# The last output block of a decoder step's down projection: token columns in three groups instead of two, and the place of one scaling

## The chip, the cores and the metric

The kernel runs on one core of a Trainium2 chip. The metric is the device time of one execution in microseconds (us), as the median of several runs. Engines are named as in the profile: PE is TensorE (PEld its weight loads), DVE is VectorE, ACT is ScalarE, POOL is GpSimd, SP is SyncE, which issues most DMAs.

## The reference, cut to what matters

The reference is one step of a hybrid decoder on 512 prompt tokens and 8 sample tokens: a mixer of mLSTM and retention heads, cross-attention, a SwiGLU block and a final RMSNorm. The change touches the end only:

```
x = x + (silu(hf @ w_gate) * (hf @ w_up)) @ w_down        # w_down: 2816 x 1024
y = x * rsqrt(mean(x * x, over the 1024 features) + EPS) * g_final
```

Tokens do not mix here: each token's row of y needs all 1024 features of its own x, and nothing of other tokens.

## The kernel before, in words

Features stand on the 128 partitions and the 520 tokens on the free axis, so the 1024 features are 8 blocks (KB) of 128 by 520. X holds the residual stream. Float32 precision comes from three products of rounded halves: high weight by high input, high weight by low input, low weight by high input. Each product has its own 128x128 stationary tile, a slice of `whi` or `wlo`, and a moving tile from A or TT (the two places that hold the 22 blocks of the SwiGLU output). Two products in a row may use the same slice of `whi`, but each is issued with a weight load of its own.

The down projection goes through its 8 output blocks in turn. Blocks 0 to 6 (L1269 to L1287) multiply both token halves, 0 to 260 and 260 to 520, and then add the result to X (L1285), square it into the running sum `ssq` (L305, L306) and scale the block by the final norm's weights (L1287). Block 7 is written apart (L1289 to L1326): 66 products (22 blocks by 3) for tokens 0 to 260, then 66 for tokens 260 to 520. The three pairs of weight chunks are kept from the first half (`chunks`). The chunks are transferred and split as before this block, in the pace of the block ahead.

When a half's products are done, generators named `finish` take over. A `finish` for a group of n tokens

- sums `ssq` over the partitions by a product with a tile of ones into `pn` (L1294),
- adds the products to X (L1295), squares block 7 (L1297) and adds that square's sum to `pn` (L1299),
- makes the reciprocal root in `rsqrt_rows`: Ln on ACT (L277), the mean `nrmv` on DVE (L278), Exp on ACT (L279), three DVE steps on `r` (L280 to L282),
- scales block 7 by the norm's weights on ACT (L1302),
- multiplies X by `r` into FR in three pieces of 3, 3 and 2 feature blocks (L1305), each followed by its DMA out, on the queues of SP, ACT and SP (L1306).

The groups that `finish` serves are given by `CUTS`: tokens 0 to 260, 260 to 390 and 390 to 520. The first half has one `finish`. The second half's 66 products serve two, which start together when the last product is done. The pieces of a `finish` are threaded between the products by `step()`. A scheduler at build time sets the order on each engine; engines keep that order when they run, and `keep_in_program_order` pins an instruction to the place where the code has it.

Of the kernel before, what the change touches and what calls it, by code (L numbers as in the profile page):

```python
# [13 lines left out]
AF = mybir.ActivationFunctionType  # L14
# [11 lines left out]
KB = 8  # L26
T = 512
NS = 8
N = T + NS
H2 = N // 2  # L30
# [23 lines left out]
V_BUF, V_WC, V_BC, V_GMIX, V_GX, V_GF, V_GM, V_GH, V_GO = 0, 24, 28, 29, 30, 31, 32, 33, 34  # L54
# [86 lines left out]
def decoder_step(ctx: ExitStack, tc: tile.TileContext, i: dict, o: list):  # L141
    nc = tc.nc
    pe, act, dve, pool, sp = nc.tensor, nc.scalar, nc.vector, nc.gpsimd, nc.sync
# [18 lines left out]
    def ps2(name):  # L162
        return acc.tile([P, 2, 512], F32, tag="acc", name=name)

    def ps1(name):
        return psums[-1].tile([P, 512], F32, tag="msc", name=name)
# [4 lines left out]
    vec = main.tile([P, KB, NV], F32, name="vec")  # L171
# [57 lines left out]
    def spawn(gen, group=None):  # L229
        tasks.append([gen, 0, group])  # L230

    def step():

        for t in list(tasks):
            t[1] -= 1
            if t[1] <= 0:
                try:
                    t[1] = next(t[0]) or 2
                except StopIteration:
                    tasks.remove(t)  # L240
# [5 lines left out]
    def proj(x, name, order=range(KB), ahead=1):  # L246
        hi, lo = W.get(ahead)
        ps = ps2(name)
        for n, k in enumerate(order):
            mm_k(ps, hi, lo, x, k, k, n == 0, n == KB - 1)  # L250
            if n % 2 and n < KB - 1:
                step()
        return ps
# [18 lines left out]
    def rsqrt_rows(pl, r, ps):  # L272

        n = ps.shape[-1]
        v = pl.tile([P, N], F32, tag="row", name="nrmv")[:, :n]
        l = pl.tile([P, N], F32, tag="row", name="nrml")[:, :n]
        act.activation(l, ps, AF.Ln, bias=eps_c, scale=1.0 / D)  # L277
        dve.tensor_scalar(v, ps, 1.0 / D, EPS, ALU.mult, ALU.add)  # L278
        act.activation(l, l, AF.Exp, scale=-0.5)  # L279
        dve.tensor_tensor(r, l, l, ALU.mult)  # L280
        dve.scalar_tensor_tensor(r, r, -0.5, v, ALU.mult, ALU.mult)
        dve.scalar_tensor_tensor(r, r, 1.5, l, ALU.add, ALU.mult)  # L282
# [85 lines left out]
    with ExitStack() as mx:  # L368
# [17 lines left out]
        n0 = mp.tile([NS, 4, HD], F32, name="n0")  # L386
# [416 lines left out]
        for hb in range(KB):  # L803
            ps = proj(A, "pgt")
# [60 lines left out]
    for ob in range(KB):  # L865

        ps = proj(B, "pwo", range(KB) if ob < KB - 1 else (*range(4, KB), *range(4)))
# [244 lines left out]
    for (k0, nk, nc_), need in zip(PASSES, (1, 2, 3)):  # L1112
        while min(done[0], attended[0]) < need or any(t[2] == "mem" for t in tasks):
            step()
        for c0 in range(0, D, nc_):
            hi, lo = W.get()
            for c in range(0, nc_, P):
                ob = (c0 + c) // P
                ps = ps2("pwc")
# [6 lines left out]
                else:  # L1126
                    xb = X[:, ob]
# [23 lines left out]
    def ff(s, k, ts):  # L1151
        return A[:, s, k, ts] if k < KB else TT[:, k - KB, s, ts]
# [55 lines left out]
    for f in range(PLAIN):  # L1208
        ps = proj(A, "pfg")
# [9 lines left out]
        ps = proj(A, "pfu", ahead=int(f < PLAIN - 1))  # L1219
# [4 lines left out]
    for f in range(PLAIN, FB):  # L1224
# [5 lines left out]
        ps = [pc, pd, ab[:, 0, :H2], ab[:, 1, :H2], pe_, cd[:, 0, :H2], cd[:, 1, :H2]]  # L1230
# [38 lines left out]
    for obs in ((0, 1), *((ob,) for ob in range(2, KB - 1))):  # L1269
# [13 lines left out]
        for ob, ps in zip(obs, pss):  # L1283
            xb = X[:, ob]
# [4 lines left out]
    xb = X[:, KB - 1]  # L1289
    chunks = []  # L1290
    def finish(ts, n, ps):

        pn = ps1("pn")[:, :n]
        pe.matmul(pn, ones, ssq[:, ts], start=True, stop=False)  # L1294
        dve.tensor_tensor(xb[:, ts], xb[:, ts], ps, ALU.add)  # L1295
        sq7 = yp.tile([P, n], F32, name="sq7", bufs=3)
        act.activation(sq7, xb[:, ts], AF.Square)  # L1297
        yield 1
        pe.matmul(pn, ones, sq7, start=False, stop=True)  # L1299
        r = yp.tile([P, n], F32, name="r", bufs=3)  # L1300
        rsqrt_rows(yp, r, pn)
        act.activation(xb[:, ts], xb[:, ts], AF.Copy, scale=vec[:, KB - 1, V_GO : V_GO + 1])  # L1302
        out = fr[:, KB * ts.start : KB * ts.stop].rearrange("p (k n) -> p k n", n=n)
        for q, k0, k1 in ((sp, 0, 3), (act, 3, 6), (sp, 6, 8)):
            dve.tensor_tensor(out[:, k0:k1], X[:, k0:k1, ts], r.unsqueeze(1).broadcast_to([P, k1 - k0, n]), ALU.mult)  # L1305
            q.dma_start(y[:, KB * ts.start + k0 * n : KB * ts.start + k1 * n].rearrange("p (k n) -> p k n", n=n), out[:, k0:k1])  # L1306

    for n0, n in ((0, H2), (H2, N - H2)):
        ts = slice(n0, n0 + n)
        ps = ps2("pfd")[:, 0, :n]  # L1310
        for k0 in range(0, FB, KB):
            if n0 == 0:
                chunks.append(W.get())
            hi, lo = chunks[k0 // KB]
            for k in range(min(KB, FB - k0)):
                for w, s in ((hi, 0), (hi, 1), (lo, 0)):
                    pe.matmul(  # L1317
                        ps, w[:, k], ff(s, k0 + k, ts),
                        start=k0 + k == 0 and w is hi and s == 0, stop=k0 + k == FB - 1 and w is lo,
                    )  # L1320
            step()
        for c0, c1 in zip(CUTS, CUTS[1:]):
            if ts.start <= c0 < ts.stop:
                spawn(finish(slice(c0, c1), c1 - c0, ps[:, c0 - ts.start : c1 - ts.start]))
        step()
    drain()  # L1326
    yx.close()
# [5 lines left out]
CUTS = (0, H2, H2 + H2 // 2, N)  # L1333
# [61 lines left out]
```

## Time and profile before

| | us |
|---|---|
| median of 3 runs (849.76 to 851.43) | 850.98 |
| the profiled execution's own time | 851.71 |
| its span, first to last instruction | 849.9 |

The span of the profile is what the views below show; 1.8 us of the profiled execution lie outside it (851.71 - 849.9). Times in the rows are counted from the start of the span. Over the whole span PE is busy 97%, DVE 74%, ACT 50%, POOL 19%. The block that the change touches is the last 27 us.

### The profile page before, as it was taken

The page shows a single profiled execution, that of the slowest core. Times are in us where ns is not written, and L with a number is a line of the kernel's source. Part 1 is how long each engine was busy: PE and PEld are TensorE (multiplying, and loading weights), DVE is VectorE, ACT ScalarE, POOL GpSimd, SP SyncE. Part 2 cuts the span into 40 slices and gives each one's busy share as a digit, 9 for nine tenths or more (in the row PEclk, how much of TensorE's full clock was granted, in tenths as well). Part 3 has the DMA queues.
Part 4 walks back from the last instruction along what each step waited for, and adds up shares of the span by engine and source line. Part 5 has one row for each costly group of instructions (what it writes and reads, how often), then busy time and mean ns, then how long its engine had stood idle before and what let it go on. Part 6 is the DMA issues. An engine that isn't in the chain of part 4 may idle for free.

```text
span 849.9 us, 16985 instructions
## 1 busy us (share of the span) xinstructions
PE 824.3 (97%) x6643; PEld 807.6 (95%) x6643; DVE 632.8 (74%) x1393; ACT 426.5 (50%) x871; POOL 163.0 (19%) x282
## 2 busy tenths in 40 slices
PE   6999999999999999899999899999999999999995
PEld 4999999999999999789999899999999999999995
DVE  5999977667676778767888899999999997422234
ACT  6556886556545544356432555555454455332231
POOL 5122422222145301424322500000000000010010
PEclk9999999999999999999999999999999999999999
DMA  8344546444526347784755222333333333333212
GB/s 279 103 131 164 176 168 217 158 138 162 189 76 216 105 127 246 235 287 130 243 196 153 75 58 93 107 113 90 109 113 118 101 99 94 94 106 94 79 59 100
DMA packets 34088, 119.01 MB, mean 140 GB/s; under 512 B 4320, under 2 KB 6560, under 8 KB 32728
## 3 DMA queue, kind: packets, MB, share of 16 engines
q1 hardware_dynamic: 27216, 95.80, 35.9%
q0 software_dynamic: 5024, 20.79, 6.7%
q10 hardware_dynamic: 1768, 1.34, 0.5%
q8 instruction: 52, 0.85, 0.4%
q14 instruction: 28, 0.23, 0.1%
HBM read 108.77 MB, written 9.14 MB: 139 GB/s over the span
## 4 chain that ended last, share of the span: by engine, by line
PE 86%; DVE 6%; DMA 4%; POOL 1%; ACT 1%; issue 1%; SPq 0%; DVEq 0%; POOLq 0%; ACTq 0%
PE pfd L1277 13%; PE pfb L1236 6%; PE pfa L1236 6%; PE pcv L222 6%; PE pgt L222 5%; PE pcq L222 5%; PE pwo L222 5%; PE ppl L222 5%; PE pwc L222 4%; PE pfd L1236 3%; PE pfe L1236 3%; PE pfc L1236 3%; PE prp L222 3%; PE pfu L222 2%; PE pfg L222 2%; PE pfd L1317 1%
## 5 line engine op out<-in xcount | busy, mean ns | idle before, releaser
L207 ACT CAST whi<-wraw 128x1024 fp32r<-128x1024 f32 (+1 forms) x104 | 107.3, 1033 | 167.3 <-PE pfd L1277 58.1
L208 DVE TENSOR_TENSOR wlo<-wraw,whi 128x1024 fp32r<-128x1024 f32 (+1 forms) x88 | 112.6, 1281 | 71.5 <-ACT whi L207 69.5
L306 POOL TENSOR_TENSOR ssq<-ssq,sq 128x520 f32<-128x520 f32 x18 | 29.1, 1618 | 355.6 <-ACT sq L305 355.5
L191 ACT CAST qhi<-wsum 128x512 fp32r<-128x512 f32 x72 | 42.9, 620 | 41.4 <-DVE wsum L1183 26.6
L1277 PE MATMUL pfd<-TT,whi 128*128 128x260 f32 x392 | 62.8, 283 | 0.0
L1277 PEld LDWEIGHTS pfd<-TT,whi 128*128 128x128 f32 x392 | 53.7, 189 | 0.0
L1236 PE MATMUL pfa<-TT,qhi 128*128 128x260 f32 x288 | 53.1, 282 | 0.0
L1236 PE MATMUL pfb<-TT,qhi 128*128 128x260 f32 x288 | 52.8, 283 | 0.0
L208 POOL TENSOR_TENSOR wlo<-wraw,whi 128x1024 fp32r<-128x1024 f32 x16 | 38.4, 2399 | 60.3 <-ACT whi L207 55.2
L191 DVE TENSOR_TENSOR qlo<-wsum,qhi 128x512 fp32r<-128x512 f32 x72 | 48.9, 683 | 0.6 <-ACT qhi L191 0.6
L222 PE MATMUL pwc<-B,whi 128*128 128x260 f32 x256 | 43.8, 287 | 4.0 <-DVE X L295 3.0
L222 PE MATMUL pcv<-A,whi 128*128 128x260 f32 x256 | 44.3, 293 | 1.7 <-ACT whi L207 1.7
L1236 PEld LDWEIGHTS pfb<-TT,qhi 128*128 128x128 f32 x288 | 44.4, 189 | 0.2 <-issue 0.2
L1236 PEld LDWEIGHTS pfa<-TT,qhi 128*128 128x128 f32 x288 | 44.4, 189 | 0.0
L222 PE MATMUL prp<-A,whi 128*128 128x260 f32 x256 | 44.2, 291 | 0.0
L222 PE MATMUL ppl<-A,whi 128*128 128x260 f32 x256 | 42.9, 287 | 0.0
L222 PE MATMUL pgt<-A,whi 128*128 128x260 f32 x256 | 42.7, 289 | 0.0
L222 PE MATMUL pcq<-A,whi 128*128 128x260 f32 x256 | 42.0, 284 | 0.0
L222 PE MATMUL pwo<-B,whi 128*128 128x260 f32 x256 | 41.4, 283 | 0.0
L1236 PE MATMUL pfb<-TT,qlo 128*128 128x260 f32 x144 | 40.8, 283 | 0.0
L222 PEld LDWEIGHTS pwc<-B,whi 128*128 128x128 f32 x256 | 35.8, 189 | 5.1 <-DVE X L295 3.7
L1236 PE MATMUL pfa<-TT,qlo 128*128 128x260 f32 x144 | 40.5, 282 | 0.0
(431 smaller groups left out, 2556.6 us busy)
## 6 DMA issues: line engine op xcount, KB each, us to landing
wraw<-in_weights_dram SPq DMA_DIRECT2D x132, 512.0 KB, 3.8
kqb<-there POOLq DMA_DIRECT2D x8, 1024.0 KB, 5.2
kv<-in_cache_k_dram SPq DMA_DIRECT2D x16, 512.0 KB, 4.3
kv<-in_cache_v_dram SPq DMA_DIRECT2D x16, 512.0 KB, 4.4
wraw<-in_weights_dram SPq DMA_DIRECT2D x8, 384.0 KB, 3.1
X<-in_x_dram SPq DMA_DIRECT2D x2, 1040.0 KB, 5.9
Cs<-in_state_C_dram POOLq DMA_DIRECT2D x4, 512.0 KB, 4.3
out_dram<-Cs POOLq DMA_DIRECT2D x4, 512.0 KB, 3.0
```

Of the source, the lines that this page charges most:

```text
L191: return act.copy(hi, src), dve.tensor_tensor(lo, src, hi.bitcast(F32), ALU.subtract)
L207: act.copy(hi[:, :n], raw[:, :n])
L208: (pool if index in LO_ON_POOL else dve).tensor_tensor(lo[:, :n], raw[:, :n], hi[:, :n].bitcast(F32), ALU.subtract)
L222: pe.matmul(ps[:m, a, :H2], w[:, k, c0 : c0 + m], x[:, s, xk, a * H2 : (a + 1) * H2], start=first and w is hi and s == 0, stop=last and w ...
L306: (dve if ob == KB - 1 else pool).tensor_tensor(ssq, ssq, s, ALU.add)
L1236: pe.matmul(out, w[:, k * P : (k + 1) * P], x[:, k * H2 : (k + 1) * H2], start=k == 0 and w is wh and x is xh, stop=k == 3 and w is wl,)
L1277: pe.matmul(ps[:, a, :H2], w[:, k - k0], ff(s, k, slice(a * H2, (a + 1) * H2)), start=k == 0 and w is hi and s == 0, stop=k == FB - 1 and ...
L1317: pe.matmul(ps, w[:, k], ff(s, k0 + k, ts), start=k0 + k == 0 and w is hi and s == 0, stop=k0 + k == FB - 1 and w is lo,)
```

## The change

Block 7 of the down projection is cut into the three groups of `CUTS` itself. Each group has its own 66 products: 66 of 260 columns, then 66 of 130, then 66 of 130. The former second half of 66 products of 260 columns becomes 132 products of 130. Every group has its own PSUM tile and its own `finish`, started when its products are done. In `finish` the ACT scaling of block 7 (L1302) is kept in program order, which puts it behind Ln and Exp.

```diff
-        act.activation(xb[:, ts], xb[:, ts], AF.Copy, scale=vec[:, KB - 1, V_GO : V_GO + 1])
+        tc.keep_in_program_order(act.activation(xb[:, ts], xb[:, ts], AF.Copy, scale=vec[:, KB - 1, V_GO : V_GO + 1]))
...
-    for n0, n in ((0, H2), (H2, N - H2)):
-        ts = slice(n0, n0 + n)
+    for c0, c1 in zip(CUTS, CUTS[1:]):
+        n0, n = c0, c1 - c0
+        ts = slice(c0, c1)
         ps = ps2("pfd")[:, 0, :n]
...
-        for c0, c1 in zip(CUTS, CUTS[1:]):
-            if ts.start <= c0 < ts.stop:
-                spawn(finish(slice(c0, c1), c1 - c0, ps[:, c0 - ts.start : c1 - ts.start]))
+        spawn(finish(ts, n, ps))
         step()
```

On PE, before, this is the very end of the program; `sq` with a number is one group's square of block 7, and the product's line is L1317.

```order
L1317 MATMUL pfd<-TT,whi 128x260 x2
L1317 MATMUL pfd<-TT,wlo 128x260
L1294 MATMUL pn<-ssq,ones 128x130 x2
L1299 MATMUL pn<-sq_10572,ones 128x130
L1299 MATMUL pn<-sq_10577,ones 128x130
```

Of the changed kernel this is the seam between the second and the third group on PE; the product's line is now L1318.

```order
L1318 MATMUL pfd<-TT,whi 128x130 x2
L1318 MATMUL pfd<-TT,wlo 128x130
L1294 MATMUL pn<-ssq,ones 128x130
L1318 MATMUL pfd<-A,whi 128x130 x2
L1318 MATMUL pfd<-A,wlo 128x130
```

The second group's first `pn` now stands ahead of the third group's 66 products, and its other one (L1299, of `sq_10572`) stands between them, behind 29 of the 66. Behind the last product only the third group's two are left.

On DVE, before, these rows follow the first group's last piece of FR; they are the two groups of 130, woven into each other.

```order
L1295 TENSOR_TENSOR X<-X,pfd 128x130 x2
L278 TENSOR_SCALAR nrmv<-pn 128x130
L280 TENSOR_TENSOR r<-nrml 128x130
L278 TENSOR_SCALAR nrmv<-pn 128x130
L281 SCALAR_TENSOR_TENSOR r<-r,nrmv 128x130
L280 TENSOR_TENSOR r<-nrml 128x130
L282 SCALAR_TENSOR_TENSOR r<-r,nrml 128x130
L281 SCALAR_TENSOR_TENSOR r<-r,nrmv 128x130
L1305 TENSOR_TENSOR FR<-X,r 128x390 x2
L1305 TENSOR_TENSOR FR<-X,r 128x260
L282 SCALAR_TENSOR_TENSOR r<-r,nrml 128x130
```

Of the changed kernel, from the same place on DVE:

```order
L1295 TENSOR_TENSOR X<-X,pfd 128x130
L278 TENSOR_SCALAR nrmv<-pn 128x130
L280 TENSOR_TENSOR r<-nrml 128x130
L281 SCALAR_TENSOR_TENSOR r<-r,nrmv 128x130
L282 SCALAR_TENSOR_TENSOR r<-r,nrml 128x130
L1305 TENSOR_TENSOR FR<-X,r 128x390 x2
L1305 TENSOR_TENSOR FR<-X,r 128x260
L1295 TENSOR_TENSOR X<-X,pfd 128x130
```

The whole chain of the second group now stands ahead of the third group's add to X, and the third group's chain, of the same rows, stands alone behind it.

## Rows read from the trace of the kernel before

**Rows 1.** The page: the span, and a group of weight loads (busy, mean ns).
```profile
span 849.9 us, 16985 instructions
L1277 PEld LDWEIGHTS pfd<-TT,whi 128*128 128x128 f32 x392 | 53.7, 189 | 0.0
```
**Rows 2.** Chain of waits from 823.4 us: start us, us, engine, tile, line, count.
```profile
823.50 7.95 PE pfd L1317 x66
...
831.88 2.97 PE pfd L1317 x25
834.85 0.45 PE pn L1299 x2
...
840.23 0.30 DVE X L1295
```
**Rows 3.** Timeline of DVE, 831.4 to 846.6 us: start us, us, instruction.
```profile
836.35 0.43 DVE L280 TENSOR_TENSOR r<-nrml 128x260 f32<-128x260 f32 x1
836.82 0.43 DVE L281 SCALAR_TENSOR_TENSOR r<-r,nrmv 128x260 f32<-128x260 f32 x1
...
837.74 2.46 DVE L1305 TENSOR_TENSOR FR<-X,r 128x780 f32<-128x780 f32 x3
840.23 0.49 DVE L1295 TENSOR_TENSOR X<-X,pfd 128x130 f32<-128x130 f32 x2
842.01 0.29 DVE L278 TENSOR_SCALAR nrmv<-pn 128x130 f32<-128x130 f32 x1 [1.29 <-ACT nrml L277]
842.28 0.29 DVE L280 TENSOR_TENSOR r<-nrml 128x130 f32<-128x130 f32 x1
...
843.56 1.37 DVE L1305 TENSOR_TENSOR FR<-X,r 128x390 f32<-128x390 f32 x3
...
845.17 1.38 DVE L1305 TENSOR_TENSOR FR<-X,r 128x390 f32<-128x390 f32 x3
```
**Rows 4.** Timeline of ACT, 839 to 847 us.
```profile
840.55 0.51 ACT L1297 ACTIVATE sq<-X 128x130 f32<-128x130 f32 x2 [4.23 <-DVE X L1295]
840.97 0.68 ACT L1302 ACTIVATE X<-X,vec 128x130 f32<-128x130 f32 x2
841.56 0.35 ACT L277 ACTIVATE nrml<-pn,vec 128x130 f32<-128x130 f32 x1
```
**Rows 5.** Timeline of PE, 839.5 to 841.7 us.
```profile
839.91 0.28 PE L1317 MATMUL pfd<-TT,wlo 128*128 128x260 f32 x1
840.03 0.61 PE L1294 MATMUL pn<-ssq,ones 128*128 128x130 f32 x4
840.91 0.71 PE L1299 MATMUL pn<-sq,ones 128*128 128x130 f32 x4 [0.28 <-ACT sq L1297]
```
**Rows 6.** Timeline of PEld, 68.4 to 69 us: loads for float32 products of 130 columns.
```profile
68.44 0.64 PEld L626 LDWEIGHTS num<-vt,w 128*128 128x128 f32 x5
```
**Rows 7.** Timeline of PEld around 272.6 us: loads for products of one column.
```profile
272.45 0.30 PEld L857 LDWEIGHTS pmn<-ones,msq 128*128 128x128 f32 x2
```
**Rows 8.** Timeline of PE, 359.1 to 360 us: products of 512 columns.
```profile
359.10 0.39 PE L214 MATMUL pmv<-whi,B 128*128 128x512 f32 x1
359.32 0.33 PE L214 MATMUL pxs<-KT,B 128*128 128x256 f32 x1
```
**Rows 9.** Busy us (and count) of PE, PEld, DVE, ACT, POOL; PEclk; DMA share, GB/s.
```profile
475.00:478.00 3.00, 1.54 (x12) 1.32 (x12) 3.00 (x2) 1.08 (x2) 2.58 (x2) 1.00 0.17 10
478.00:480.50 2.50, 1.26 (x10) 1.26 (x11) 2.50 (x5) 1.26 (x2) 0.03 (x1) 1.00 0.52 198
480.50:484.00 3.50, 3.50 (x19) 3.50 (x18) 3.41 (x4) 3.35 (x5) 3.30 (x2) 0.51 0.00 0
823.30:831.30 8.00, 8.00 (x69) 8.00 (x68) 0.70 (x1) 1.37 (x2) 1.31 (x1) 1.00 0.01 2
```
**Rows 10.** Timeline of PE, 480.9 to 482 us.
```profile
480.99 1.07 PE L222 MATMUL pfg<-A,whi 128*128 128x260 f32 x4
481.85 0.42 PE L222 MATMUL pfg<-A,wlo 128*128 128x260 f32 x1
```

## The prediction

> **What bounds the kernel now.** I read the page first: it gives the span of 849.9 us [rows 1]. The profiled execution took 851.71 us, 1.8 more than its span and 0.73 more than the median of the three runs, 850.98. The working below is a difference within the span, and I add it to the median at the end.
>
> Then the chain of waits over the last 27 us. The reader is to see two stretches. Up to about 840 us the chain is PE and nothing else: 66 products of the first half in 7.95 us, 25 products of the second in 2.97 us [rows 2]. That is 0.1205 and 0.119 us from one start to the next; I take 0.1195. From 840.23, the add of the last products to X, the chain is one long `finish` on DVE and ACT with PE nearly idle. DVE writes its last piece at 845.17 + 1.38 = 846.55 [rows 3], and 3.35 us from there to 849.9 are the last DMA's issue and landing and the program's end. So there are two prices: a product more on PE costs its spacing, and each step of the last `finish` costs its length.
>
> Third the timelines, engine by engine, for what one step takes [rows 3 to 5], and last other stretches of the kernel for what a narrow product costs [rows 6 to 8], which the last block does not show.
>
> **Part 1: 132 narrow products for 66 wide ones.** The columns are the same in sum; the number of products and of weight loads doubles. The 66 wide ones take 66 x 0.1195 = 7.89 us. No product of rounded halves with 130 columns occurs in the trace, so I bound it from rows.
>
> - From above, and nearest: float32 products of 130 columns, each pass with a fresh 128x128 tile. Five loads last 0.64 us together and one lasts 0.19 [rows 1, 6], so they start (0.64 - 0.19) / 4 = 0.112 us apart.
> - What paces those could be the columns or the load. Products of one column settle it: two loads in 0.30 us start 0.11 us apart though there is nothing to stream [rows 7]. A fresh full tile costs 0.11 us, however few the columns.
> - From below, if loads were hidden: products of 512 columns start 0.22 us apart [rows 8], those of 260 columns 0.1195. That is 0.1005 us for 252 columns, 0.0004 each, and 130 columns fewer than 260 would give 0.068 us.
> - Beyond the first: no saving at all, 0.12 us as now.
>
> I take 0.112 us. The load's 0.19 us is the same length in the last block as in rows 6 and 7, so I see no reason why it should overlap more there. 132 x 0.112 = 14.78 us, and the first term is 14.78 - 7.89 = **+6.9 us**. Its ends are 132 x 0.068 - 7.89 = +1.1 and 132 x 0.12 - 7.89 = +7.95.
>
> A page of the Trainium skill speaks against this size. "TensorE: Matmul & The Clock Gate", section "Back-to-back issue gap", gives about 81 ns per product for a stream of loads and products of 128 columns. By it the term would be 132 x 0.081 - 7.89 = +2.8 us. Rows 6 and 7 show 0.11 for loads of float32 tiles, so I leave it to the rivals.
>
> **Part 2: the second group's sums of squares on PE.** Before, the four passes of the two L1294 products follow the last product, from 840.03, and lie beside the add on DVE; those of L1299 come at 840.91 [rows 5]. Now the second group's L1294 and L1299 (two passes each) stand ahead of the last product. At 0.112 us a pass [rows 6] that is 4 x 0.112 = **+0.45 us**. I see no wait there: L1299 stands behind 29 products of the third group, 29 x 0.112 = 3.2 us, and its square is ready 0.32 us of add and about 0.4 us of ACT after the add to X starts [rows 3, 4].
>
> The last product's start thus moves by 6.9 + 0.45 = +7.35 us, and the third group's add to X with it, from 840.23 to about 847.6 (from the last product's start to the add it is 840.23 - 839.91 = 0.32 us now [rows 5]; a narrow one may end 0.05 us sooner, which I leave in the range).
>
> **Part 3: what the second group's `finish` hides.** It now runs beside the third group's products. It has to be over before the third group's add to X, since that add is queued behind its last piece on DVE. The first group's last piece ends at 837.74 + 2.46 = 840.20 now [rows 3], and its L1299 follows 25 products that become narrow (25 x 0.0075 = 0.2 us sooner), so DVE is free at about 840.0, when the second group's products are through. L1299 of the second group starts at about 843.0; Ln follows 0.6 us behind (841.56 - 840.91, less what is in part 5), `nrmv` 0.45 behind Ln (842.01 - 841.56), and the own chain of part 4 takes 1.23 + 1.38 us. The end is 846.65, 0.9 us ahead of 847.6. So nothing is added, and it is the place to look if the sum is too small.
>
> **Part 4: a `finish` alone at the end.** Two shares of the woven chain go. From `nrmv` to the first piece of FR it is 843.56 - 842.01 = 1.55 us now. Alone it would be 842.28 - 842.01 = 0.27 for the first step, which does not wait for `nrmv`, and three steps that wait for each other. With 260 columns such a step starts 836.82 - 836.35 = 0.47 behind the one before, 0.04 above its length 0.43; with 130 columns that makes 0.28 + 0.04 = 0.32 [rows 3]. 0.27 + 3 x 0.32 = 1.23, which saves 0.32. And the second set of pieces goes: 846.55 less the end of the first set, 843.56 + 1.37 = 844.93, is 1.62 [rows 3]. Together **-1.94 us**. The DMAs of the last three pieces are as many and as large as now, so the 3.35 us behind them stay; the second group's DMAs have been out for four microseconds by then.
>
> **Part 5: scaling behind Exp.** On ACT two scalings stand between the squares and Ln: 0.68 us from 840.97, while Ln could start only when L1299's first product is through. Ln starts 841.56, just when ACT is done with them [rows 4]; the second pass of L1299 starts some 0.2 us behind 840.91 and lasts 0.27 (0.61 less three starts of 0.112 [rows 5]), so it ends at 841.4, and Ln could start 0.1 us behind that: the edit takes 0.05 us. In the changed kernel one scaling of 0.39 us (the first of the two) would fit into that wait anyway. Behind Exp it ends well over 1 us ahead of the third piece of FR, which alone needs it. **-0.05 us**, bounds 0 and -0.1.
>
> **The sum.** 6.9 + 0.45 - 1.94 - 0.05 = **+5.4 us**. The span becomes 855.3, an execution like the profiled one 857.1, and the median 850.98 + 5.4 = **856.4 us**. With 0.12 us a product it is 1.05 + 0.03 more, 857.4; the runs of before lie 1.2 us below and 0.5 us above their median.
>
> **The rivals.**
>
> *Loads hidden, narrow products paced by their columns (not slower).* For it: with 260 columns the spacing, 0.1195, is no larger than columns explain, and loads overlap products everywhere. Against it: rows 7, where there are no columns to hide behind. At 0.068 us the products of all groups are over by 842.5, but DVE now decides: the first group's last piece ends at 840.2 - 25 x 0.0515 = 838.9, and then two chains of add to X, square, sum, root and pieces follow one another in DVE's order, each 0.69 + 0.59 + 0.45 + 1.23 + 1.38 = 4.34 us (840.91 - 840.23 = 0.69 up to L1299; the rest as above). That ends at 847.6, 1.0 us behind 846.55: 852.0 us, within 0.2% of now: 6 in 100. DVE takes over from PE when the spacing is below about 0.1 us. By the page's 81 ns the same working gives the first group's end at 839.25 and 1.4 us more in all, 852.4 us; since rows 6 and 7 show none of it, 2 in 100. The order on DVE also says that the change can hardly be faster: products that cost nothing would still leave the two chains in a row.
>
> *The clock falls in the narrow groups (much slower).* For it: the array would stream columns for about half of each 0.112 us, and the granted clock did fall once in this trace: PE was busy 1.54 of 3 us and 1.26 of 2.5 us up to 480.5, and the next 3.5 us ran at 0.51, about 1.2 GHz [rows 9]. Products of 260 columns then start 0.86 / 4 = 0.215 us apart [rows 10]. Against it: PE stood still there, and the profile will count it busy in the narrow groups, as it does now, at 1.00 [rows 9]. If it held for all 132 products: 132 x (0.215 - 0.112) = 13.6 us more, 870 us; a fall late in the third group costs 1 or 2 us. 5 in 100.
>
> *No gain at the end.* The scheduler could have woven the groups again so that the third group's chain is no shorter. The order of the changed program shows them apart, so this needs the second `finish` to be late by more than the 0.9 us of part 3. A stall of 2 us there gives 857.5, inside the range. 3 in 100.
>
> **How the numbers follow.** The forecast has 84 in 100, with its own range from 855.2 to 857.8 (0.107 to 0.12 us a product, and the spread of the runs). 0.2% of 850.98, about what a measurement of this kernel can tell from no change, is 1.7 us: slower means above 852.7. The forecast, the fallen clock and the late `finish` are all slower, 92 in 100; hidden loads are within 0.2% for the most part, and with a low median they could be a gain: 6 and 2. To leave out no more than 2 in 10 the range goes down toward the hidden loads and up past a late fall of the clock: 853.6 to 858.8.
>
> **What would show it.** Right, if the starts of 66 products of 130 columns lie 7.4 us apart in sum and weight loads start 0.11 us apart; if the third group's add to X starts near 847.6, with DVE idle just ahead of it; and if from that add to the last piece's end it is 4.3 us where it is 6.3 now. Wrong, if narrow products start under 0.1 us apart, if the add to X of the third group follows the second group's last piece without a gap, or if PEclk is below 1.00 while products run.

## The result, and the profile after

| | before | after |
|---|---|---|
| median of 6 runs, us | 851.29 (849.76 to 853.66) | 856.82 (855.44 to 859.1) |
| profiled execution, us | 851.71 | 855.71 |
| its span, us | 849.9 | 853.9 |

The ratio is 1.0061, with a 95% interval from 1.0038 to 1.0083. That is slower by well under 1%, 5.5 us between the medians, where 856.4 us and +5.4 were forecast.

The spans differ by 4.0 us only. The chain of waits of the changed kernel (columns as in [rows 2]) shows why: it reaches the block with 1.35 us less behind it, the row of the second group's first products at 830.53 where it was 831.88 [rows 2]. No engine's order of work differs ahead of the block, and the six other kernels below, with the same order up to there, reach this row between 829.90 and 834.05 us. So I take the 1.35 us as the spread between executions.

```profile
830.53 2.74 PE pfd L1318 x25
833.28 0.49 PE pn L1299 x2
833.76 4.53 PE pfd L1318 x41
838.29 0.27 PE pn L1294 x2
838.57 3.19 PE pfd L1318 x29
841.75 0.27 PE pn L1299 x2
842.03 4.09 PE pfd L1318 x37
...
846.14 0.30 DVE X L1295
```

Read from its own start the block is clear. From that row to the last group's add to X it took 840.23 - 831.88 = 8.35 us [rows 2]; now it takes 846.14 - 830.53 = 15.61, **+7.26**. From that add to the end of the span it took 849.9 - 840.23 = 9.7 us; now 853.9 - 846.14 = 7.8, **-1.9**. Together +5.35 us.

The loads of PEld in the third group set the pace. Each row merges neighbours; the two that count 2 start 0.33 us apart with three loads begun, and two loads last 0.30, as in [rows 7].

```profile
838.63 0.30 PEld L1318 LDWEIGHTS pfd<-A,whi 128*128 128x128 f32 x2
838.85 0.19 PEld L1318 LDWEIGHTS pfd<-A,wlo 128*128 128x128 f32 x1
838.96 0.30 PEld L1318 LDWEIGHTS pfd<-A,whi 128*128 128x128 f32 x2
```

The DVE timeline (start us, us, instruction), which answers to [rows 3], shows the ends of the two narrow `finish` chains one behind the other. The second group's last piece ends at 843.86 + 1.38 = 845.24, and DVE waits 0.91 us for the third group's products (in brackets: idle before it, and what ended that).

```profile
843.86 1.38 DVE L1305 TENSOR_TENSOR FR<-X,r 128x390 f32<-128x390 f32 x3
846.14 0.29 DVE L1295 TENSOR_TENSOR X<-X,pfd 128x130 f32<-128x130 f32 x1 [0.91 <-PE pfd L1318]
847.76 0.29 DVE L278 TENSOR_SCALAR nrmv<-pn 128x130 f32<-128x130 f32 x1 [1.33 <-ACT nrml L277]
848.11 0.29 DVE L280 TENSOR_TENSOR r<-nrml 128x130 f32<-128x130 f32 x1
...
849.10 1.38 DVE L1305 TENSOR_TENSOR FR<-X,r 128x390 f32<-128x390 f32 x3
```

On ACT, which answers to [rows 4], Ln comes 0.89 us behind the square's start with nothing of ACT's in between, and the scaling stands behind Exp.

```profile
846.47 0.31 ACT L1297 ACTIVATE sq<-X 128x130 f32<-128x130 f32 x1 [3.34 <-DVE X L1295]
847.36 0.37 ACT L277 ACTIVATE nrml<-pn,vec 128x130 f32<-128x130 f32 x1 [0.58 <-PE pn L1299]
847.76 0.31 ACT L279 ACTIVATE nrml<-nrml 128x130 f32<-128x130 f32 x1
847.98 0.39 ACT L1302 ACTIVATE X<-X,vec 128x130 f32<-128x130 f32 x1
```

The granted clock (seventh figure behind the stretch, columns as in [rows 9]) stayed at 1.00, which is 2.4 GHz, through both narrow groups:

```profile
830.40:838.10 7.70, 7.70 (x69) 7.64 (x68) 3.71 (x8) 1.72 (x4) 0.00 (x0) 1.00 0.00 0
838.30:846.10 7.80, 7.80 (x71) 7.80 (x71) 3.12 (x9) 1.29 (x4) 0.00 (x0) 1.00 0.44 166
```

### The profile page after: what moved, and what is told of

Read it like the earlier page. It is cut to its first block, busy times and chain, and to the rows that moved or that the text cites. A ratio compares the mean times of both kernels' runs of the same rounds, so it can differ in the third digit from the quotient of the medians.

```text
span 853.9 us, 17116 instructions
## 1 busy us (share of the span) xinstructions
PE 831.1 (97%) x6709; PEld 815.2 (95%) x6709; DVE 632.1 (74%) x1393; ACT 426.4 (50%) x871; POOL 160.7 (19%) x282
## 3 DMA queue, kind: packets, MB, share of 16 engines
q10 hardware_dynamic: 1768, 1.34, 0.5%
## 4 chain that ended last, share of the span: by engine, by line
PE 87%; DVE 5%; DMA 3%; POOL 2%; issue 1%; ACT 1%; SPq 0%; DVEq 0%; POOLq 0%
PE pfd L1277 13%; PE pfb L1236 6%; PE pfa L1236 6%; PE pcv L222 6%; PE pgt L222 5%; PE pcq L222 5%; PE ppl L222 5%; PE pwo L222 5%; PE pwc L222 4%; PE prp L222 4%; PE pfd L1236 3%; PE pfe L1236 3%; PE pfc L1236 3%; PE pfd L1318 3%; PE pfg L222 2%; PE pfu L222 2%
```

## Experiments

The theory is that 66 more loads of a full float32 tile at 0.112 us, less what they let go in wide products, cost 6.9 us, and that 1.9 us come back at the end. Its rivals are a pace set by columns, a pace set by a fixed cost per product, and a loss by the second edit. The profiles of all kernels are compared over the last block: from the chain's row of the second group's first products (behind the first group's L1294) to the last group's add, and from there to the end of the span. The page gives the span to 0.1 us, so the last two sums are good to about 0.1 us.

| kernel | products, us | add to end, us | block, us | ratio to before (95%) |
|---|---|---|---|---|
| before | 8.35 | 9.7 | 18.1 | 1 |
| after | 15.61 | 7.8 | 23.4 | 1.0061 (1.0038 to 1.0083) |
| scale_behind_exp | 8.34 | 10.0 | 18.3 | 0.9992 (0.9964 to 1.0020) |
| three_parts_alone | 15.61 | 7.6 | 23.2 | 1.0062 (1.0039 to 1.0084) |
| cut_200_60 | 17.70 | 6.5 | 24.2 | 1.0071 (1.0046 to 1.0095) |
| one_load_hi_lo | 10.98 | 9.4 | 20.4 | 1.0020 (0.9994 to 1.0046) |
| bf16_views | 8.96 | 7.6 | 16.6 | 0.9983 (0.9940 to 1.0026) |
| one_finish_260 | 8.34 | 10.5 | 18.8 | 1.0002 (0.9973 to 1.0030) |

**The second edit alone (scale_behind_exp)**

```diff
-        act.activation(xb[:, ts], xb[:, ts], AF.Copy, scale=vec[:, KB - 1, V_GO : V_GO + 1])
+        tc.keep_in_program_order(act.activation(xb[:, ts], xb[:, ts], AF.Copy, scale=vec[:, KB - 1, V_GO : V_GO + 1]))
```

> The kernel before with the second edit alone: the ACT scaling (L1302) kept behind Ln and Exp, two halves of 66 products as before. My theory (the edit is worth 0 to 0.1 us, the whole change of time is the 66 more products): within 0.2% of the kernel before, and from the two groups' add to X to the end of the last piece of FR 6.2 to 6.4 us, where it was 6.32. Rival (the scaling was on the path and its move hides a larger loss elsewhere): at least 0.4 us less there, one scaling of 0.39 us.

No change in time can be told. From the adds to the last piece's end the trace has 843.37 + 1.38 - 838.24 = 6.51 us, 0.19 more than before, so the rival is out and my bound of 6.4 was missed too. The DVE timeline shows how:

```profile
838.24 0.49 DVE L1295 TENSOR_TENSOR X<-X,pfd 128x130 f32<-128x130 f32 x2
...
841.43 1.37 DVE L1305 TENSOR_TENSOR FR<-X,r 128x390 f32<-128x390 f32 x3
842.72 0.29 DVE L281 SCALAR_TENSOR_TENSOR r<-r,nrmv 128x130 f32<-128x130 f32 x1
843.04 0.29 DVE L282 SCALAR_TENSOR_TENSOR r<-r,nrml 128x130 f32<-128x130 f32 x1
843.37 1.38 DVE L1305 TENSOR_TENSOR FR<-X,r 128x390 f32<-128x390 f32 x3
```

With one more pin on ACT the two chains are woven in another way on DVE, an engine that the edit does not name: both last steps on `r` of the second chain now stand behind the first chain's pieces, 843.37 - 841.43 = 1.94 us from pieces to pieces where it was 845.17 - 843.56 = 1.61 [rows 3]. What the first chain gains is less than that.

**The three groups alone (three_parts_alone)**

```diff
-        tc.keep_in_program_order(act.activation(xb[:, ts], xb[:, ts], AF.Copy, scale=vec[:, KB - 1, V_GO : V_GO + 1]))
+        act.activation(xb[:, ts], xb[:, ts], AF.Copy, scale=vec[:, KB - 1, V_GO : V_GO + 1])
```

> The changed kernel without the second edit: three groups with products of their own, the scaling again ahead of Ln. My theory: the same as the changed kernel within 0.1 us in the last block (23.9 us from the first sums of squares to the end of the span), 0.4 to 0.8% above the kernel before in time. Rival (the scaling's new place costs or saves something here): the last block differs by 0.3 us or more from the changed kernel's.

The chain has the same 15.61 us of products, from 830.41 to 846.02:

```profile
830.41 2.74 PE pfd L1318 x25
...
846.02 0.30 DVE X L1295
```

The block differs from the changed kernel's by 0.17 us, all of it behind the last piece of FR, where only the DMA's landing and the program's end are left. That is over the 0.1 I allowed and under the rival's 0.3, and up to that piece the two kernels agree within 0.01 us. Nothing of the change's cost or gain belongs to the second edit; the ratio is the same.

**Other columns, as many loads (cut_200_60)**

```diff
-CUTS = (0, H2, H2 + H2 // 2, N)
+CUTS = (0, H2, H2 + 200, N)
```

> The changed kernel with groups of 260, 200 and 60 tokens in place of 260, 130 and 130. My theory (a fresh stationary tile sets the pace of a narrow product, 0.112 us whatever its columns): products of 200 and of 60 columns both start 0.112 us apart, so the products take as long as in the changed kernel; the last finish gets shorter with 60 columns (about 3.2 us from the add to the last piece's end, where it is 4.34), of which the longer finish of 200 in front of it may take 0.2 back; last block about 0.9 us shorter than the changed kernel's, still 4 to 5 us over the kernel before. Rival (columns and a fixed share set the pace, 0.0004 us a column through the 0.1195 us of 260 and the 0.112 of 130): products of 200 columns start 0.116 apart and those of 60 near 0.108. Rival (columns alone, through 512 and 260): 0.096 and 0.04.

On PE, products of 200 columns start 0.11 us apart (838.21 to 838.55 for three, 841.57 - 838.21 = 3.36 us for 30), and those of 60 do so too (843.18 to 843.51 for three, 845.19 - 843.18 = 2.01 us for 18):

```profile
838.21 0.28 PE L1318 MATMUL pfd<-TT,wlo 128*128 128x200 f32 x1
838.33 0.39 PE L1318 MATMUL pfd<-TT,whi 128*128 128x200 f32 x2
838.55 0.28 PE L1318 MATMUL pfd<-TT,wlo 128*128 128x200 f32 x1
...
841.57 0.28 PE L1318 MATMUL pfd<-TT,wlo 128*128 128x200 f32 x1
```
```profile
843.18 0.28 PE L1318 MATMUL pfd<-A,wlo 128*128 128x60 f32 x1
843.29 0.39 PE L1318 MATMUL pfd<-A,whi 128*128 128x60 f32 x2
843.51 0.28 PE L1318 MATMUL pfd<-A,wlo 128*128 128x60 f32 x1
...
845.19 0.27 PE L1318 MATMUL pfd<-TT,wlo 128*128 128x60 f32 x1
```

So columns do not set the pace: 60 cost what 200 cost, 0.112 us each, where columns with a fixed share would have made it 0.108 and 0.116. The time, though, is a miss: the block was to be 0.9 us shorter than the changed kernel's and is 0.8 longer. The clock fell in the 60 columns. The windows before and after 847.6 show PE and PEld busy without a gap in both, and PEclk 1.00 and then 0.50 (1.2 GHz):

```profile
841.90:847.60 5.70, 5.70 (x52) 5.70 (x50) 1.62 (x5) 1.52 (x4) 0.00 (x0) 1.00 0.44 168
847.60:851.90 4.30, 4.30 (x22) 4.30 (x21) 2.50 (x6) 0.00 (x0) 0.00 (x0) 0.50 0.50 191
```
```profile
848.75 0.40 PE L1318 MATMUL pfd<-TT,wlo 128*128 128x60 f32 x1
848.96 0.61 PE L1318 MATMUL pfd<-TT,whi 128*128 128x60 f32 x2
849.39 0.40 PE L1318 MATMUL pfd<-TT,wlo 128*128 128x60 f32 x1
```

At the lower level three products start in 0.64 us, 0.21 each, as in [rows 10]. The trace has 18 products at this spacing: 18 x 0.10 = 1.8 us more, about the whole miss of 1.7. All ten timed runs of this kernel have a mean granted clock of 0.987 to 0.991; the ten of three_parts_alone have 0.993 to 0.998. A mean does not tell where in the run the clock was low: this kernel's profiled run, but not the changed kernel's, also has a stretch at 0.51 near 135 us. So the fall in the last block is shown for the profiled run; for the other nine it is likely, not shown.

**Fewer loads, the same columns (one_load_hi_lo)**

```diff
+                if n0:
+                    x2 = A[:, :, k0 + k, ts] if k0 + k < KB else TT[:, k0 + k - KB, :, ts]
+                    both = lambda: pe.matmul(pw, hi[:, k], x2, start=k0 + k == 0, stop=k0 + k == FB - 1)
...
+                    pe.matmul(ps, lo[:, k], ff(0, k0 + k, ts), start=False, stop=False)
...
-        dve.tensor_tensor(xb[:, ts], xb[:, ts], ps, ALU.add)
+        for z in ps:
+            dve.tensor_tensor(xb[:, ts], xb[:, ts], z, ALU.add)
```

> The changed kernel with fewer loads for the same columns in the two narrow groups: the two products that share a slice of whi (high and low input, 130 columns each) become one of 260 columns into neighbouring PSUM columns; the group has 22 products of 260 and 22 of 130 where it had 66 of 130, and its finish adds two PSUM pieces to X. My theory (loads set the pace): a pair starts 0.23 us after the pair before (0.1195 + 0.112) where three products took 0.336, so the two groups' products take 10.2 us in place of 14.8, and the last product starts 4.5 us sooner. The build-time order weaves the two finishes into each other again, so the end costs about as much as before, 6 to 6.6 us, and the whole is 2 to 4 us over the kernel before. Rival (columns set the pace): the same columns take the same time, 14.8 us, and the whole is slower than the changed kernel.

A pair of products, 260 and 130 columns, starts 0.24 us behind the last one (840.07 to 840.31):

```profile
840.07 0.23 PE L1324 MATMUL pfd<-A,wlo 128*128 128x130 f32 x1
840.13 0.34 PE L1321 MATMUL pfd<-A,whi 128*128 128x260 f32 x1
840.31 0.23 PE L1324 MATMUL pfd<-A,wlo 128*128 128x130 f32 x1
```
```profile
840.07 0.19 PEld L1321 LDWEIGHTS pfd<-A,whi 128*128 128x128 f32 x1
840.18 0.19 PEld L1324 LDWEIGHTS pfd<-A,wlo 128*128 128x128 f32 x1
840.31 0.19 PEld L1321 LDWEIGHTS pfd<-A,whi 128*128 128x128 f32 x1
```
```profile
833.05 0.44 PE pn L1294 x2
...
844.47 0.61 DVE L1296 TENSOR_TENSOR X<-X,pfd 128x130 f32<-128x130 f32 x2 [2.44 <-PE pfd L1321]
```

The products of the two groups take 10.98 us (from 833.05 + 0.44 to the first add of the last group at 844.47) instead of 15.61, 4.6 less, with as many columns streamed. A third of the loads are gone, and the time goes with them. A third of the products are gone too, so the sum alone does not tell a load from a fixed cost per product; the starts do. A product of 130 columns is followed by the next after only 0.06 us (840.07 to 840.13), and that one after 0.18, while the loads start 0.11 and 0.13 us apart. The even pace is the loads', not the products'. The block is 2.3 us over the kernel before, within the 2 to 4 expected; by time, 1.002 with an interval that holds 1, it cannot be told from it.

**The same products on smaller tiles (bf16_views)**

```diff
+                    wk_, xk = w[:, k], ff(s, k0 + k, ts)
+                    if n0:
+                        wk_, xk = (z.bitcast(mybir.dt.bfloat16)[:, 1::2] for z in (wk_, xk))
                     pe.matmul(
-                        ps, w[:, k], ff(s, k0 + k, ts),
+                        ps, wk_, xk,
```

> The changed kernel with as many products of as many columns in the two narrow groups, but a smaller stationary tile in bytes: weights and inputs are read as bfloat16, the upper halves of the same words (this leaves out the lower halves of both). My theory (the loading of a float32 tile sets 0.112 us): the load is seen shorter than 0.19 us, products start well under 0.1 us apart, near the 0.068 that columns alone give, and from the first sums of squares to the last product's start it is 9.5 to 11 us where it was 15.9. The time is then set by the two finishes on DVE, 0.5 to 2.5 us over the kernel before. Rival (a fixed cost of each product, whatever it loads): 0.112 us stays, 15.9 us stays, the time stays at the changed kernel's.

The load is 0.097 us long (min/median/max in ns below) instead of 0.19, and three products start in 0.18 us, 0.06 each:

```profile
L1321 PEld LDWEIGHTS <-whi x88: 95/97/100, 833.5 to 842.4; 128*128 128x128 bf16 x88
```
```profile
834.36 0.22 PE L1321 MATMUL pfd<-A,wlo 128*128 128x130 bf16 x1
834.42 0.28 PE L1321 MATMUL pfd<-A,whi 128*128 128x130 bf16 x2
834.54 0.22 PE L1321 MATMUL pfd<-A,wlo 128*128 128x130 bf16 x1
```

So no fixed cost of a product holds the pace at 0.112: with as many products of as many columns it falls to 0.06 when the operands get smaller. The tile loaded and the input streamed both changed here; that the load is the one that counts is shown by the two kernels above together, by the columns of the first and the starts of the second. The load changed in more than its size: the trace records its weights as read in 32 x 4 elements a row, those of a float32 load as 128 in one piece. Whether the fewer bytes or this form made it shorter is not shown. From the first sums of squares to the last product's start it is 9.3 us, just under the 9.5 to 11 expected. The expected time was a miss on the good side: the block is 16.6 us, 1.5 *less* than in the kernel before, where 0.5 to 2.5 more were expected; by the time of the runs the two cannot be told apart. The chain gives the block's start, and the DVE timeline shows why:

```profile
833.87 1.84 PE pfd L1321 x31
```
```profile
842.83 0.29 DVE L1295 TENSOR_TENSOR X<-X,pfd 128x130 f32<-128x130 f32 x1 [0.32 <-PE pfd L1321]
843.03 1.37 DVE L1305 TENSOR_TENSOR FR<-X,r 128x390 f32<-128x390 f32 x3
```

The third group's add now stands ahead of the second group's pieces, which so lie beside the third group's square and sum. With other products the program was put into another order when it was built.

**One chain instead of two woven ones (one_finish_260)**

```diff
-CUTS = (0, H2, H2 + H2 // 2, N)
+CUTS = (0, H2, N)
```

> Two groups of 260 tokens, each with 66 products and one finish: no narrow products and no finish of 130 at all, so the two woven chains of the kernel before become one chain of 260. My theory (the kernel before loses nothing by its two half groups and wins little): products as before, 0.1195 us apart, 8.63 us from the first sums of squares to the last product's start; from the add to the end of the last piece 6.4 us where it was 6.32, and the larger last DMA lands 0.2 to 0.4 us later; in all 0.2 to 0.6 us over the kernel before, not to be told from it by time. Rival (the weaving of two chains is what the end costs, so one chain is shorter): 5.5 us or less from the add to the last piece's end.

```profile
839.44 0.42 DVE L1295 TENSOR_TENSOR X<-X,pfd 128x260 f32<-128x260 f32 x1
...
843.52 2.46 DVE L1305 TENSOR_TENSOR FR<-X,r 128x780 f32<-128x780 f32 x3
```

This kernel has the second edit too. From the add to the last piece's end it is 843.52 + 2.46 - 839.44 = 6.54 us, 0.2 over the two woven chains of the kernel before and the same as the 6.51 of scale_behind_exp, which weaves two with that edit; and 0.5 us more go behind the last piece, whose DMA is twice as large. The block is 0.7 us longer, a little more than expected; the time cannot be told from the kernel before's. The weaving is not what the end costs.

None of these points to a version with the reference's precision that beats the kernel before: of those with three groups the one with fewer loads comes nearest, and its block is still 2.3 us longer.

## Why the prediction was right

The mechanism was right part by part, as the profile's 5.35 us for 5.4 shows. That the medians came within 0.1 us of the forecast too is more than they can show: by the interval of the ratio the difference is 3.2 to 7.1 us.

*Part 1, the products.* Right. Two groups of 66 at 0.112 us were forecast from loads of float32 tiles [rows 6, 7]. In the changed kernel 41, 29 and 37 products take 4.53, 3.19 and 4.09 us in the chain, 0.110 each. The rule of the Trainium skill that would have made this term +2.8 us ("TensorE: Matmul & The Clock Gate", section "Back-to-back issue gap": about 81 ns for products of 128 columns) does not hold for these tiles: 0.11 measured with float32 words, 0.06 with bfloat16, one on either side of it.

*Part 2, the sums of squares ahead of the last product.* Right within 0.1 us together with part 1: +7.26 where 7.35 were forecast. There is no wait for the square.

*Part 3, the hidden `finish`.* Right: it was to end 0.9 us ahead of the third group's add, and DVE waited 0.91 us.

*Part 4, the end.* Right in sum, 849.10 + 1.38 - 846.14 = 4.34 us for 4.34. Steps inside were off and made up for each other: Ln comes 0.52 us behind L1299 (846.84 in the chain), not 0.59; `nrmv` comes 0.40 us behind Ln, not 0.45; and the first step on `r` waits for Exp's end, not for DVE, so that the pieces start 1.34 us behind `nrmv` instead of 1.23. That the sum is exact to 0.01 us is luck. Behind the last piece 853.9 - 850.48 = 3.42 us are left, not the 3.35 held fixed.

*Part 5, the second edit.* The term of -0.05 us was nothing: with and without it the changed kernel has the same chain. Alone on the kernel before it was 0.19 us the other way, outside my bounds of 0 and -0.1, since I priced the pin only on ACT.

*The rivals.* Hidden loads are excluded by cut_200_60 and one_load_hi_lo. But a sentence of that rival failed: that products which cost nothing would still leave the two chains in a row. bf16_views shows the block 1.5 us shorter than before, because the order on DVE is not fixed against the products' cost. The price of 852.0 us holds only for the order I had in front of me. The fallen clock did not come at 130 columns in the profiled run, but my reason against it, that PE had stood still where the clock fell [rows 9], was too narrow: at 60 columns it fell with PE counted busy throughout.

## What to carry to other kernels

Splitting a block of products over columns to hide the work behind it costs one more load per product, and a product costs the larger of its load and its columns: here 0.112 us for the load against 0.1195 us for 260 columns, so groups of less than about 240 columns, an estimate (0.112 / 0.1195 x 260 = 244), pay for what they do not use. Weigh that against what is hidden, here 7 us against 2. And price an edit in the order that the build makes of it: a pin on one engine, or cheaper products, can reorder another.

## What was not expected

The granted clock fell from 2.4 to 1.2 GHz at 847.6 us in cut_200_60 after 5.7 us of products of 60 columns, with no gap in PE's busy time, and the products' starts went from 0.11 to 0.21 us apart. Products of 130 columns, at the same spacing, kept 1.00 for 15 us. What made the difference was not tried further.
